# A hand-made order for the first projection of a hybrid encoder layer, its norm row spread by TensorE, and table powers moved from GpSimd to VectorE

## The chip, the cores and the metric

The kernel runs on one core of a Trainium2 chip. The metric is the device time of one execution in microseconds (us); the median of three runs is compared.

## The reference

One encoder layer is applied to a prompt of 256 and a sample of 1024 tokens, with a model width of 1024. Each row is normalized and projected by `w_in` into eight parts. `xs` goes through a bidirectional state-space mixer, q, k and v through differential attention; the rest are gates. Cut to what the change touches:

```python
h = x * rsqrt(mean(x * x) + eps) * norm_g            # (1280 tokens, 1024)
proj = h @ w_in                                      # xs, zs, q, k, v, za, gs, ga
A_bar = exp(A * dt)                                  # 2 directions, 32 groups, 64 states, complex
B_bar = (A_bar - 1) / A * B
h_f, h_b = scans with A_bar over (B_bar @ xs)        # forward and backward
y = real(C[0] @ h_f + C[1] @ h_b) + d_skip * xs
```

The kernel works in blocks of eight tokens. So it needs the powers of A_bar up to the eighth, and tables of the phase of A_bar to the eighth at each of 160 block positions. These tables are built as products of a low table (16 entries, `Tlr`, `Tli`) and a high one (10 entries, `Thr`, `Thi`).

## The kernel before

All matrix products are made of three fp32r products: each operand is split into a high part (a cast on ScalarE) and a low part (the rest, by a subtraction on VectorE or GpSimd).

The program goes through these phases. First the value projection: ten tiles of 128 tokens are loaded (`load_x`), normalized (`norm_x`), transposed on TensorE into `hTh` and `hTl` (`trans_x`), and multiplied by the value weights `Wvh` and `Wvl`, which come in four blocks of 128 columns (`load_wv`). The result goes through `vh` and `vl` to DRAM. The norm takes the sum of squares on ScalarE, some steps of one column on VectorE with a power on GpSimd between them (`rstd_newton`, L189 to L194), and one wide product with the row `gB`, which holds `norm_g` in all 128 partitions, loaded by a broadcast DMA. Second comes the xs projection (L572 to L586), third q and k with the rotary products (L605 to L630). Then follow the scans, attention, and the output stage.

Beside the first three phases a generator, `prep_gen`, makes the tables and the small matrices of the state-space part, one stretch of it at each `step_prep`. Its first part holds exponentials, sine and cosine, powers, and the tables; here `cmul(G, ...)` is six operations on GpSimd. Its loop of 16 rounds (from L390) begins behind the value projection, since its pool `prepl` stands on memory that this phase gives back. Each round makes `Bb` (GpSimd, L395 to L397), from it `Bm` (ScalarE, L401), `wbp` and `wc` (VectorE), four transposes of `wbp` (L413), small products with `Bb` and `Bm` (L435, L438), `kt`, and the wide table `tt` (GpSimd, L470).

A planner puts the instructions of every engine in order at build time, by priorities in program order and its own estimate of durations; on the chip each engine then works in that order and waits where an operand is late. `tc.issue_after(ins)` puts what is traced in it behind `ins` on the same engine. `tc.manual_schedule()` keeps the program's own order, on all engines or on those that are named; the scan phase already uses it for TensorE and SyncE. SyncE issues nearly all DMAs.

The pools that matter: `x` has three buffers, `vh` and `vl` one each, `wst` (raw weights) two, and `wh` and `wl` two each. PSUM has two banks for matmuls and two for transposes.

Of the kernel before, what the change touches and what calls it, by code (L numbers as in the profile page):

```python
# [11 lines left out]
F32 = mybir.dt.float32  # L12
F32R = mybir.dt.float32r
I32 = mybir.dt.int32
AF = mybir.ActivationFunctionType
ALU = mybir.AluOpType
AX = mybir.AxisListType
PSUM = bass.MemoryType.PSUM

D = 1024  # L20
KD = 8
DH = 512
# [21 lines left out]
PREPN = 2  # L44
PREP1 = 2
TTV = 0
GP = 1
O_XS, O_ZS, O_Q, O_K, O_V, O_ZA, O_GS, O_GA = 0, 512, 1024, 1536, 2048, 2560, 3072, 4096

# [60 lines left out]
def cmul(eng, o_re, o_im, a_re, a_im, b_re, b_im, t, u):  # L110
    eng.tensor_tensor(t, a_im, b_im, op=ALU.mult)
    eng.tensor_tensor(u, a_im, b_re, op=ALU.mult)
    eng.tensor_tensor(o_im, a_re, b_im, op=ALU.mult)
    eng.tensor_tensor(o_im, o_im, u, op=ALU.add)
    eng.tensor_tensor(u, a_re, b_re, op=ALU.mult)
    eng.tensor_tensor(o_re, u, t, op=ALU.subtract)
# [9 lines left out]
def kernel(  # L126
# [85 lines left out]

    wdma = [None]

    def w_stage(col, q=None):
        st = wp.tile([128, KD, 128], F32, tag="wst", name="wst")
        wdma[0] = (q or SP).dma_start(st, w_in_v[:, :, col:col + 128])
        return st

# [33 lines left out]
    def prep_gen():  # L253
# [79 lines left out]
        G.tensor_tensor(Gi, Gi, rc, op=ALU.mult)  # L333
        yield
        ua, ub = (cs, sn), (sc("ubr"), sc("ubi"))
        for _ in range(3):
            cmul(G, ub[0], ub[1], ua[0], ua[1], ua[0], ua[1], t1, t2)
            ua, ub = ub, ua
        ur, ui = ua
        uni = sc("uni")  # L340
        G.tensor_scalar(uni, ui, -1.0, None, op0=ALU.mult)
        Hr, Hi = sc("Hr"), sc("Hi")
        cmul(G, Hr, Hi, Gr, Gi, ur, uni, t1, t2)
        G.tensor_copy(ui[64:128], uni[64:128])
        yield
        Br = pp.tile([128, NG, GC], F32, name="Br")
        Bi = pp.tile([128, NG, GC], F32, name="Bi")
# [10 lines left out]
        for tr_, ti_, cnt in ((Tlr, Tli, 16), (Thr, Thi, 10)):  # L358
            G.memset(tr_[:, :, 0:1], 1.0)
            G.memset(ti_[:, :, 0:1], 0.0)  # L360
            n = 1
            while n < cnt:
                m = min(n, cnt - n)
                cmul(G, tr_[:, :, n:n + m], ti_[:, :, n:n + m], tr_[:, :, 0:m], ti_[:, :, 0:m],
                     bc(ur, 2, m), bc(ui, 2, m), bt[:, :, :m], bu[:, :, :m])
                cmul(G, wr, wi, ur, ui, ur, ui, t1, t2)
                ur, wr = wr, ur
                ui, wi = wi, ui
                n *= 2
                yield  # L370
# [108 lines left out]
    def step_prep(n=1, loop=True):  # L479
        for _ in range(n):  # L480
            if in_loop[0] and not loop:
                return
            if next(prep, None) == "loop":
                in_loop[0] = True

    with ExitStack() as p0:
        xp = p0.enter_context(tc.tile_pool(name="xp", bufs=2, reuse_waits="tile"))
        vp = p0.enter_context(tc.tile_pool(name="vp", bufs=1, reuse_waits="tile"))
        Wvh = vp.tile([128, KD, DH], F32R, name="Wvh")
        Wvl = vp.tile([128, KD, DH], F32R, name="Wvl")  # L490
        gB = vp.tile([128, D], F32, name="gB")
        xt = {}

        def load_x(i):
            t = xp.tile([128, D], F32, tag="x", name="x", bufs=3)
            for rs, src in x_rows(i):
                wdma[0] = SP.dma_start(t[rs], src)
            xt[i] = t

        xns = {}  # L500

        def norm_x(i):
            t = xt.pop(i)
            xn = xp.tile([128, D], F32, tag="xn", name="xn", bufs=2)
            ss = xp.tile([128, 1], F32, tag="ss", name="ss")
            r = xp.tile([128, 1], F32, tag="r", name="r")
            A.activation(xn, t, AF.Square, accum_out=ss)
            rstd_newton(xp, r, ss, D, EPS, "n")
            V.scalar_tensor_tensor(xn, t, r[:, 0:1], gB, op0=ALU.mult, op1=ALU.mult)
            xns[i] = xn  # L510

        def trans_x(i):
            xn = xns.pop(i)
            for hf in range(2):
                ps = tr_bank()
                for s in range(4):
                    k = hf * 4 + s
                    PE.transpose(ps[:, s * 128:(s + 1) * 128], xn[:, k * 128:(k + 1) * 128], ident)
                pv = ps.rearrange("p (k n) -> p k n", n=128)
                hs = (slice(None), slice(hf * 4, hf * 4 + 4), slice(i * 128, i * 128 + 128))  # L520
                A.copy(hTh[hs], pv)
                V.tensor_tensor(hTl[hs], pv, hTh[hs], op=ALU.subtract)

        def load_wv(b):
            st = w_stage(O_V + b * 128)
            A.copy(Wvh[:, :, b * 128:(b + 1) * 128], st)
            V.tensor_tensor(Wvl[:, :, b * 128:(b + 1) * 128], st, Wvh[:, :, b * 128:(b + 1) * 128], op=ALU.subtract)

        load_x(0)
        SP.dma_start(gB, norm_g[0:1].broadcast_to([128, D]))  # L530
        load_wv(0)
        load_wv(1)
        norm_x(0)
        trans_x(0)
        load_x(1)
        load_wv(2)
        load_wv(3)
        first = wdma[0]
        norm_x(1)
        for i in range(10):  # L540
            if i + 2 < 10:
                with tc.issue_after(first.ins):
                    load_x(i + 2)
                norm_x(i + 2)
            if i + 1 < 10:
                trans_x(i + 1)
            ps = mm_bank()
            tk = slice(i * 128, i * 128 + 128)
            hw = 256 if i < 2 else DH
            for c in range(0, DH, hw):  # L550
                cc = slice(c, c + hw)
                for k in range(KD):
                    PE.matmul(ps[:, cc], hTh[:, k, tk], Wvh[:, k, cc], start=(k == 0), stop=False)
                    PE.matmul(ps[:, cc], hTh[:, k, tk], Wvl[:, k, cc], start=False, stop=False)
                    PE.matmul(ps[:, cc], hTl[:, k, tk], Wvh[:, k, cc], start=False, stop=(k == KD - 1))
            vh = xp.tile([128, DH], F32R, tag="vh", name="vh", bufs=1)
            vl = xp.tile([128, DH], F32R, tag="vl", name="vl", bufs=1)
            A.copy(vh, ps)
            V.tensor_tensor(vl, ps, vh, op=ALU.subtract)
            for d_, s_ in ((vh_d, vh), (vl_d, vl)):  # L560
                SP.dma_start(d_[:, :, i, :].rearrange("h p e -> p h e"), s_.bitcast(F32).rearrange("p (h e) -> p h e", h=NH))
            with tc.issue_after(wdma[0].ins):
                step_prep(PREPN, False)

    with ExitStack() as p1:
        rp = p1.enter_context(tc.tile_pool(name="rp", bufs=1, reuse_waits="tile"))
# [620 lines left out]
```

## Time and profile before

| | us |
|---|---|
| median of 3 runs | 1134.97 |
| lowest and highest | 1134.88, 1136.84 |
| profiled execution | 1136.67 |
| its span, first to last instruction | 1134.9 |
| TensorE matmuls busy in it | 1069.3 |
| VectorE busy | 787.2 |
| ScalarE busy | 463.0 |
| GpSimd busy | 385.3 |

The rows below come from the profiled execution. PE is TensorE, PEld its weight loads, DVE VectorE, ACT ScalarE, POOL GpSimd, SPq the DMA issues of SyncE. An instruction row gives its start, its duration, the engine, the line, the operation with the tile it writes and the tiles it reads, partitions x elements, and a count; in brackets stands the idle time of the engine before it and what ended it. Consecutive matmuls overlap, so their pace is read from start to start.

### The profile page before, as it was taken

To read this page: it belongs to the slowest core of one execution; us is meant where nothing else is said; L and a number is where in the kernel's file an instruction comes from. 1 tells how busy PE (TensorE), PEld (TensorE's weight loads), DVE (VectorE), ACT (ScalarE), POOL (GpSimd) and SP (SyncE) were. 2 spreads that over 40 slices of the span, in tenths; PEclk is the share of its full clock that TensorE was granted. 3 is DMA by queue.
4 is the path that set the end of the run, shared out by engine and by line. 5 is a ranking of instruction groups with operands and counts; after the bars stand their busy time and mean duration, and the time that the engine had idled before them with its cause. 6 is when DMAs were issued, how large, how long until landed. Compare 5 with 4: busy or idle time off the path is not lost.

```text
span 1134.9 us, 18049 instructions
## 1 busy us (share of the span) xinstructions
PE 1069.3 (94%) x6475; PEld 989.2 (87%) x6475; DVE 787.2 (69%) x1458; ACT 463.0 (41%) x927; POOL 385.3 (34%) x551
## 2 busy tenths in 40 slices
PE   5998899999989999899999999999999999998997
PEld 4886677788889898799999998999999999998997
DVE  5856986997859999577678677766342676666524
ACT  4542332233212221355555555645453444544332
POOL 1499899922023323222122122222141003520032
PEclk8999899999998999999999999999999999999998
DMA  7934454555486765814525516311635974569212
GB/s 221 232 109 143 119 157 150 167 181 165 146 267 201 212 183 153 236 48 118 154 67 136 157 47 176 112 47 52 216 120 175 291 228 123 161 192 267 57 57 93
DMA packets 186297, 174.11 MB, mean 153 GB/s; under 512 B 32736, under 2 KB 161760, under 8 KB 186208
## 3 DMA queue, kind: packets, MB, share of 16 engines
q1 hardware_dynamic: 150880, 144.65, 43.2%
q10 hardware_dynamic: 35328, 28.32, 7.8%
q8 instruction: 51, 0.84, 0.3%
q14 instruction: 38, 0.31, 0.1%
HBM read 114.23 MB, written 58.69 MB: 152 GB/s over the span
## 4 chain that ended last, share of the span: by engine, by line
PE 45%; DVE 19%; DMA 7%; issue 4%; ACT 3%; POOL 3%; SPq 0%; POOLq 0%; ACTq 0%; DVEq 0%
PE mm L647 5%; PE mm L646 5%; PE mm L648 5%; DVE z L738 3%; DVE z L737 3%; PE xb L994 2%; PE xb L995 2%; PE xb L996 2%; PE tr L1127 2%; PE tr L1128 2%; PE tr L1129 2%; PE mm L245 2%; PE mm L247 2%; PE mm L246 2%; PE S L860 2%
## 5 line engine op out<-in xcount | busy, mean ns | idle before, releaser
L646 PE MATMUL mm<-hTh,wh 128*128 128x424 f32 (+1 forms) x576 | 213.0, 370 | 10.8 <-ACT zo L652 10.8
L648 PE MATMUL mm<-hTh,wl 128*128 128x424 f32 (+1 forms) x576 | 206.7, 359 | 0.0
L647 PE MATMUL mm<-hTl,wh 128*128 128x424 f32 (+1 forms) x576 | 206.6, 359 | 0.0
L646 PEld LDWEIGHTS mm<-hTh,wh 128*128 128x128 f32 x576 | 109.5, 190 | 17.4 <-ACT zo L652 13.0
L245 PE MATMUL mm<-hTh,wh 128*128 128x512 f32 (+1 forms) x288 | 107.5, 373 | 7.8 <-ACT xo L580 5.5
L647 PEld LDWEIGHTS mm<-hTl,wh 128*128 128x128 f32 x576 | 109.8, 191 | 4.6
L648 PEld LDWEIGHTS mm<-hTh,wl 128*128 128x128 f32 x576 | 109.5, 190 | 3.3
L864 DVE TENSOR_REDUCE mx<-S 128x1 f32<-128x1024 f32 (+1 forms) x80 | 84.3, 1058 | 38.8 <-PE S L862 38.5
L875 POOL TENSOR_SCALAR p<-p,rs 128x1024 f32<-128x1024 f32 (+1 forms) x40 | 41.5, 1037 | 202.2 <-DVE rs L873 196.3
L239 POOL TENSOR_TENSOR wl<-wst,wh 128x1024 fp32r<-128x1024 f32 x24 | 64.1, 2672 | 126.9 <-ACT wh L238 55.5
L246 PE MATMUL mm<-hTl,wh 128*128 128x512 f32 (+1 forms) x288 | 106.1, 368 | 0.0
L247 PE MATMUL mm<-hTh,wl 128*128 128x512 f32 (+1 forms) x288 | 104.2, 362 | 0.0
L868 ACT ACTIVATE p<-S,mx 128x1024 f32<-128x1024 f32 (+1 forms) x80 | 79.2, 993 | 59.9 <-DVE mx L865 47.1
L1127 PE MATMUL tr<-wqh,mh 128*128 128x256 f32 x320 | 89.7, 281 | 2.3 <-DVE o L1131 2.3
L1128 PE MATMUL tr<-wql,mh 128*128 128x256 f32 x320 | 89.2, 279 | 0.0
L1129 PE MATMUL tr<-wqh,ml 128*128 128x256 f32 x320 | 89.0, 279 | 0.0
L245 PEld LDWEIGHTS mm<-hTh,wh 128*128 128x128 f32 x288 | 55.3, 192 | 18.0 <-ACT xo L580 6.5
L1134 POOL TENSOR_TENSOR o<-o,finB 128x256 f32<-128x256 f32 x30 | 28.1, 938 | 104.9 <-ACT jk L1133 104.9
L1127 PEld LDWEIGHTS tr<-wqh,mh 128*128 128x128 f32 x320 | 60.1, 188 | 3.3 <-DVE o L1131 3.3
L246 PEld LDWEIGHTS mm<-hTl,wh 128*128 128x128 f32 x288 | 55.5, 193 | 8.6
L247 PEld LDWEIGHTS mm<-hTh,wl 128*128 128x128 f32 x288 | 55.2, 192 | 8.8
L1128 PEld LDWEIGHTS tr<-wql,mh 128*128 128x128 f32 x320 | 60.1, 188 | 0.0
(392 smaller groups left out, 2809.5 us busy)
## 6 DMA issues: line engine op xcount, KB each, us to landing
wst<-in_w_in_dram ACTq DMA_DIRECT2D x24, 512.0 KB, 3.9
wst<-in_w_in_dram SPq DMA_DIRECT2D x16, 512.0 KB, 5.5
wst<-in_w_branch_dram SPq DMA_DIRECT2D x32, 256.0 KB, 4.8
wqs<-in_w_out_dram SPq DMA_DIRECT2D x16, 512.0 KB, 4.3
tt_d<-tt SPq DMA_DIRECT2D x16, 320.0 KB, 2.6
tb<-tt_d SPq DMA_DIRECT2D x8, 640.0 KB, 4.5
zt<-gs_d SPq DMA_DIRECT2D x16, 320.0 KB, 4.1
x<-in_x_sample_dram SPq DMA_DIRECT2D x8, 512.0 KB, 5.1
```

The lines of the kernel that those rows point to most:

```text
L239: e.tensor_tensor(lv, st, hv, op=ALU.subtract)
L245: PE.matmul(ps[:, :n], wh[:, k, :], hTh[:, k, c0:c0 + n], start=(k == 0), stop=False)
L246: PE.matmul(ps[:, :n], wh[:, k, :], hTl[:, k, c0:c0 + n], start=False, stop=False)
L247: PE.matmul(ps[:, :n], wl[:, k, :], hTh[:, k, c0:c0 + n], start=False, stop=(k == KD - 1))
L646: PE.matmul(ps[:, :n], wh[:, k, :], hTh[:, k, c0:c0 + n], start=(k == 0), stop=False)
L647: PE.matmul(ps[:, :n], wh[:, k, :], hTl[:, k, c0:c0 + n], start=False, stop=False)
L648: PE.matmul(ps[:, :n], wl[:, k, :], hTh[:, k, c0:c0 + n], start=False, stop=(k == KD - 1))
L864: V.tensor_reduce(mx, S[:, :nk], axis=AX.X, op=ALU.max)
L868: A.activation(p[:, :nk], S[:, :nk], AF.Exp, bias=mx, scale=1.0 / math.sqrt(HD), accum_out=sm[:, t:t + 1])
L1127: PE.matmul(ps[:, :256], mh[:, k, ts_], oh_[:, k], start=(k == 0), stop=False)
L1128: PE.matmul(ps[:, :256], mh[:, k, ts_], ol_[:, k], start=False, stop=False)
L1129: PE.matmul(ps[:, :256], ml[:, k, ts_], oh_[:, k], start=False, stop=(k == 7))
```

## The change

The value projection is written out in a fixed order. Up to the split of the last weight block, all engines keep program order; behind that TensorE and SyncE do, and the others are planned, behind that split. The four weight blocks are asked for at once (two of them in the buffers of `wh` and `wl`), as are four x tiles. Block 1's low part is made on GpSimd. The first two tiles are multiplied by halves of the columns, the low halves first. `norm_g` is loaded as one row and spread over the partitions by two matmuls with a row of ones. There are 24 matmuls of `ones_e` with itself ahead of these and 30 behind, whose results nobody reads. The store of a tile's values is issued one round later, and `vh` and `vl` get two buffers. In `prep_gen` the three squarings and all powers for the low and the high table run on VectorE with temporaries of their own.

```diff
+WARM = 30
@@ prep_gen
+        v1, v2 = sc("v1"), sc("v2")
         for _ in range(3):
-            cmul(G, ub[0], ub[1], ua[0], ua[1], ua[0], ua[1], t1, t2)
+            cmul(V, ub[0], ub[1], ua[0], ua[1], ua[0], ua[1], v1, v2)
...
-        G.tensor_scalar(uni, ui, -1.0, None, op0=ALU.mult)
+        V.tensor_scalar(uni, ui, -1.0, None, op0=ALU.mult)
         Hr, Hi = sc("Hr"), sc("Hi")
         cmul(G, Hr, Hi, Gr, Gi, ur, uni, t1, t2)
-        G.tensor_copy(ui[64:128], uni[64:128])
+        sgn = sc("sgn")
+        V.tensor_copy(sgn[0:64], ui[0:64])
+        V.tensor_copy(sgn[64:128], uni[64:128])
+        u1r, u1i = sc("u1r"), sc("u1i")
+        V.tensor_copy(u1r, ur)
+        ur, ui, ub = u1r, sgn, (ur, ui)
...
-                cmul(G, tr_[:, :, n:n + m], ti_[:, :, n:n + m], tr_[:, :, 0:m], ti_[:, :, 0:m],
+                cmul(V, tr_[:, :, n:n + m], ti_[:, :, n:n + m], tr_[:, :, 0:m], ti_[:, :, 0:m],
                      bc(ur, 2, m), bc(ui, 2, m), bt[:, :, :m], bu[:, :, :m])
-                cmul(G, wr, wi, ur, ui, ur, ui, t1, t2)
+                cmul(V, wr, wi, ur, ui, ur, ui, v1, v2)
@@ value projection
-            t = xp.tile([128, D], F32, tag="x", name="x", bufs=3)
+            t = xp.tile([128, D], F32, tag="x", name="x", bufs=4)
...
-            V.scalar_tensor_tensor(xn, t, r[:, 0:1], gB, op0=ALU.mult, op1=ALU.mult)
+            w = D // 2 if i == 0 else D
+            for c in range(0, D, w):
+                V.scalar_tensor_tensor(xn[:, c:c + w], t[:, c:c + w], r[:, 0:1], gB[:, c:c + w], op0=ALU.mult,
+                                       op1=ALU.mult)
...
+        def split_wv(b, e):
+            st = wvs.pop(b)
             A.copy(Wvh[:, :, b * 128:(b + 1) * 128], st)
+            return e.tensor_tensor(Wvl[:, :, b * 128:(b + 1) * 128], st, Wvh[:, :, b * 128:(b + 1) * 128],
+                                   op=ALU.subtract)
...
-        SP.dma_start(gB, norm_g[0:1].broadcast_to([128, D]))
...
+        with tc.manual_schedule(engines={EN.PE, EN.SP}):
+            with tc.manual_schedule():
+                load_x(0)
+                g1 = xp.tile([1, D], F32, name="g1", bufs=1)
+                SP.dma_start(g1, norm_g[0:1])
+                wvs[0] = w_stage(O_V)
+                wvs[1] = w_stage(O_V + 128)
+                load_x(1)
+                wvs[2] = w_stage(O_V + 256, tag="wh")
+                wvs[3] = w_stage(O_V + 384, tag="wl")
+                load_x(2)
+                load_x(3)
+                one1 = xp.tile([1, 128], F32, name="one1", bufs=1)
+                V.memset(one1, 1.0)
+                junk = ps_w.tile([128, 512], F32, tag="junk", name="junk")
+                for _ in range(24):
+                    PE.matmul(junk[:, :128], ones_e, ones_e, start=True, stop=True)
+                for c in range(0, D, 512):
+                    ps = tr_bank()
+                    PE.matmul(ps, one1, g1[:, c:c + 512], start=True, stop=True)
+                    V.tensor_copy(gB[:, c:c + 512], ps)
+                for _ in range(WARM):
+                    PE.matmul(junk[:, :128], ones_e, ones_e, start=True, stop=True)
+                norm_x(0)
+                split_wv(0, V)
+                trans_x(0)
+                split_wv(1, G)
+                norm_x(1)
+                pss = [mm_bank()]
+                v_half(pss[0], 0, lo)
+                trans_x(1)
+                pss.append(mm_bank())
+                v_half(pss[1], 1, lo)
+                split_wv(2, V)
+                first = split_wv(3, V)
+            after_v = lambda: tc.issue_after(first.ins)
+            pend = []
+            for i in range(10):
+                if i + 4 < 10:
+                    load_x(i + 4)
+                with after_v():
+                    if i + 2 < 10:
+                        norm_x(i + 2)
+                    if 2 <= i + 1 < 10:
+                        trans_x(i + 1)
+                    if i < 2:
+                        v_half(pss[i], i, hi)
+                        ps = pss[i]
+                    else:
+                        ps = mm_bank()
+                        v_half(ps, i, slice(0, 512))
+                    pend.append(v_evict(ps, i))
+                    step_prep(PREPN, False)
+                if i:
+                    v_store(*pend.pop(0))
+            v_store(*pend.pop(0))
```

`v_half` makes the 24 matmuls of a tile over the given columns, `v_evict` the cast to `vh` and the subtraction to `vl`, and `v_store` the two stores; their bodies are those of the loop before.

## Rows read from the trace of the kernel before

**Rows 1.** Stretches: length, PE, PEld, DVE, ACT, POOL busy; granted clock, DMA share, GB/s

```profile
49.30:87.40 38.10, 38.08 (x184) 31.01 (x185) 20.63 (x44) 17.10 (x33) 37.91 (x116) 1.00 0.41 120
...
97.50:131.00 33.50, 24.42 (x118) 19.22 (x115) 27.87 (x46) 11.85 (x29) 29.38 (x63) 0.85 0.39 119
```

**Rows 2.** TensorE's waits, 86 to 231 us, and its wait for wbp, 96 to 126

```profile
PE tr L413 <- DVE wbp L116: 7.8, 3, 4.6
PE mm L245 <- ACT xo L580: 5.5, 3, 2.7
PE mm L245 <- DVE m L613: 2.3, 2, 1.8
PE tr L438 <- ACT Bm L401: 1.1, 1, 1.1
...
PE tr L413 <- DVE wbp L116: 6.5, 2, 4.6
```

**Rows 3.** ScalarE's longest wait, 86 to 231 us (total, times, longest)

```profile
ACT Bm L401 <- POOL Bb L116: 61.9, 11, 8.2
```

**Rows 4.** Timeline of a handover between GpSimd, ScalarE and VectorE

```profile
96.10 0.25 POOL L116 TENSOR_TENSOR Bb<-s,s 128x32 f32<-128x32 f32 x1
...
96.38 0.59 ACT L401 ACTIVATE Bm<-Bb,hmask 128x64 f32<-128x64 f32 x2 [8.17 <-POOL Bb L116]
...
98.82 3.03 DVE L239 TENSOR_TENSOR wl<-wst,wh 128x1024 fp32r<-128x1024 f32 x1 [3.94 <-ACT wh L238]
```

**Rows 5.** Timeline of the start, all engines

```profile
1.46 0.23 DVE L165 TENSOR_SCALAR ones_e<-ident 128x128 fp32r<-128x128 f32 x1
...
6.30 0.15 DVE L189 TENSOR_SCALAR nm<-ss 128x1 f32<-128x1 f32 x1 [4.61 <-ACT xn L507]
...
7.97 1.29 DVE L509 SCALAR_TENSOR_TENSOR xn<-x,r,gB 128x1024 f32<-128x1024 f32 x1
...
8.37 1.04 ACT L526 CAST Wvh<-wst 128x1024 fp32r<-128x1024 f32 x1 [2.10 <-DMA wst<-in_w_in_dram]
...
9.40 1.94 PE L518 MATMUL tr<-ident,xn 128*128 128x128 f32 x8 [9.40 <-DVE xn L509]
...
23.29 0.56 PE L554 MATMUL mm<-Wvl,hTh 128*128 128x256 f32 x1
...
23.64 0.41 PE L555 MATMUL mm<-Wvh,hTl 128*128 128x256 f32 x1
...
23.86 0.41 PE L553 MATMUL mm<-Wvh,hTh 128*128 128x256 f32 x1
...
30.00 0.28 PE L554 MATMUL mm<-Wvl,hTh 128*128 128x256 f32 x1
30.12 0.28 PE L555 MATMUL mm<-Wvh,hTl 128*128 128x256 f32 x1
```

**Rows 6.** GpSimd's timeline, a small and a wide table product, and a split

```profile
77.35 0.24 POOL L112 TENSOR_TENSOR t<-wi,wr 128x32 f32<-128x32 f32 x1
...
83.42 0.64 POOL L113 TENSOR_TENSOR Tli<-Tlr,wi 128x256 f32<-128x256 f32 x1
...
281.05 2.38 POOL L239 TENSOR_TENSOR wl<-wst,wh 128x1024 fp32r<-128x1024 f32 x1 [4.87 <-ACT wh L238]
```

**Rows 7.** VectorE's timeline, small and wide products

```profile
45.47 0.18 DVE L63 SCALAR_TENSOR_TENSOR xep<-xep,xer 128x32 f32<-128x32 f32 x1
45.57 0.18 DVE L101 TENSOR_TENSOR scsq<-scsq,scm 128x32 f32<-128x32 f32 x1
...
91.98 0.46 DVE L428 TENSOR_TENSOR d<-PCi,Cr 128x256 f32<-128x256 f32 x1
...
126.44 0.42 DVE L115 TENSOR_TENSOR e<-Fr,Br 128x256 f32<-128x256 f32 x1
...
130.16 0.95 DVE L111 TENSOR_TENSOR e<-Fi,Bi 128x256 f32<-128x256 f32 x1
```

**Rows 8.** TensorE's timeline, two fp32 products of 256 columns

```profile
174.67 1.13 PE L438 MATMUL tr<-wc,Bm 128*128 128x256 f32 x4
```

More of the change, by code (lines that the diff above doesn't have):

```diff
@@ L213, with w_stage @@
     wdma = [None]
-    def w_stage(col, q=None):
-        st = wp.tile([128, KD, 128], F32, tag="wst", name="wst")
+    def w_stage(col, q=None, tag="wst"):
+        st = wp.tile([128, KD, 128], F32, tag=tag, name="wst")
         wdma[0] = (q or SP).dma_start(st, w_in_v[:, :, col:col + 128])
@@ L492 @@
         xt = {}
+        ps_w = p0.enter_context(tc.tile_pool(name="ps_w", bufs=1, space=PSUM, reuse_waits="tile"))
+        EN = mybir.EngineType
         def load_x(i):
-            t = xp.tile([128, D], F32, tag="x", name="x", bufs=3)
+            t = xp.tile([128, D], F32, tag="x", name="x", bufs=4)
             for rs, src in x_rows(i):
@@ L522, in trans_x @@
                 V.tensor_tensor(hTl[hs], pv, hTh[hs], op=ALU.subtract)
-        def load_wv(b):
-            st = w_stage(O_V + b * 128)
+        def split_wv(b, e):
+            st = wvs.pop(b)
             A.copy(Wvh[:, :, b * 128:(b + 1) * 128], st)
-            V.tensor_tensor(Wvl[:, :, b * 128:(b + 1) * 128], st, Wvh[:, :, b * 128:(b + 1) * 128], op=ALU.subtract)
-        load_x(0)
-        SP.dma_start(gB, norm_g[0:1].broadcast_to([128, D]))
-        load_wv(0)
-        load_wv(1)
-        norm_x(0)
@@ L534 @@
[L534 to L547, printed above, removed]
-            tk = slice(i * 128, i * 128 + 128)
[L549 to L557, printed above, removed]
+            return e.tensor_tensor(Wvl[:, :, b * 128:(b + 1) * 128], st, Wvh[:, :, b * 128:(b + 1) * 128],
+                                   op=ALU.subtract)
@@ new lines, in v_half, with v_evict @@
+        def v_half(ps, i, cc):
+            tk = slice(i * 128, i * 128 + 128)
+            for k in range(KD):
+                PE.matmul(ps[:, cc], hTh[:, k, tk], Wvh[:, k, cc], start=(k == 0), stop=False)
+                PE.matmul(ps[:, cc], hTh[:, k, tk], Wvl[:, k, cc], start=False, stop=False)
+                PE.matmul(ps[:, cc], hTl[:, k, tk], Wvh[:, k, cc], start=False, stop=(k == KD - 1))
+        def v_evict(ps, i):
+            vh = xp.tile([128, DH], F32R, tag="vh", name="vh", bufs=2)
+            vl = xp.tile([128, DH], F32R, tag="vl", name="vl", bufs=2)
@@ L558, with v_store @@
             A.copy(vh, ps)
             V.tensor_tensor(vl, ps, vh, op=ALU.subtract)
+            return i, vh, vl
+        def v_store(i, vh, vl):
             for d_, s_ in ((vh_d, vh), (vl_d, vl)):
                 SP.dma_start(d_[:, :, i, :].rearrange("h p e -> p h e"), s_.bitcast(F32).rearrange("p (h e) -> p h e", h=NH))
-            with tc.issue_after(wdma[0].ins):
-                step_prep(PREPN, False)
+        wvs = {}
+        lo, hi = slice(0, 256), slice(256, 512)
+        with tc.manual_schedule(engines={EN.PE, EN.SP}):
[54 more added lines that the diff above has]
+            v_store(*pend.pop(0))
```

## Prediction

> **What bounds the kernel now.** I read the busy time by stretches first, then TensorE's list of waits, then the waits of ScalarE, and last the timelines around the stops. The first 87 us belong to the value projection, 87 to 176 to the xs projection, 176 to 309 to q and k; everything behind that is untouched and only shifts. In the projections TensorE is nearly always at work; what can be won are its stops. Two places have them.
>
> The first is the start: the first transposes come at 9.40, and the run without stops begins only with the matmul at 23.29 [rows 5]. From there to 87.4 TensorE is busy in 38.08 of the last 38.1 us [rows 1], so this phase has no other gap to give back.
>
> The second is the xs projection. From 97.5 to 131 TensorE is busy 24.42 of 33.5 us [rows 1], and its waits from 86 to 231 add up to 16.7 us [rows 2]. The releasers named are VectorE (wbp, 7.8 us), ScalarE (xo, 5.5 us; Bm, 1.1 us) and VectorE again (m, 2.3 us). Behind them stands GpSimd. ScalarE runs in order and waits 61.9 us in 11 waits for GpSimd's Bb, to make Bm [rows 3]. The handover shows how this spreads: Bb ends at 96.35, Bm starts at 96.38, the cast of the next weights sits behind it on ScalarE, and VectorE has idled 3.94 us when it can begin its half of the split at 98.82, which takes 3.03 us [rows 4]; its wbp products come after that. GpSimd is late because it is full: 37.91 of 38.1 us busy from 49.3 to 87.4, and 29.38 of 33.5 from 97.5 on [rows 1], and the power tables lie in its queue ahead of and between the Bb.
>
> **The change, part by part.** *Powers on VectorE.* Removed from GpSimd: 18 products of three squarings, one negation, one half copy, and eight rounds of the tables, each with 6 small products and 6 table products. That is 68 operations of 128x32 at 0.24 us, 16.3 us, and table products of 32, 64, 128 and 256 columns (12, 18, 12 and 6 of them). With 0.24 us at 32 and 0.64 at 256 columns [rows 6], and straight lines between (0.30 and 0.41, estimates), they take 2.9 + 5.4 + 4.9 + 3.8 = 17.0 us. GpSimd's queue gets 33 us shorter, and Bb no longer waits behind it.
>
> On VectorE the 128x32 operations start 0.10 us apart, and 128x256 takes 0.42 [rows 7]. Its share is 70 small ones, 7.0 us, and 1.2 + 2.6 + 2.8 + 2.5 = 9.1 us of table products (0.144 and 0.24 for 64 and 128 columns, estimates between the same ends): 16.1 us. They land between 49.3 and 87.4, where VectorE is idle 38.1 - 20.63 = 17.5 us [rows 1]; this slack hides them. Without it they would cost TensorE up to 16 us. Beside GpSimd the price grows: a 128x256 product takes 0.46 us beside its small operations and 0.95 beside the wide ones [rows 7]. In this stretch GpSimd has mostly small ones, so I take 0.46 / 0.42, a factor 1.1: 17.7 us. That fills the slack to the brim, and since the tables are wanted only later, I charge 1 us (between 0 and the 19.5 us of the slower rival below).
>
> The Trainium skill, "GPSIMD Engine Reference", section "Key points", says that the engine shares its SBUF interfaces with VectorE and contends with VectorE instructions that read two SBUF inputs, which all the moved products do. The trace agrees for the wide operations: 0.95 against 0.42 us [rows 7]. If it held as fully for the narrow ones, the sum would be that of rival D.
>
> *What the xs phase gets back.* Of TensorE's 16.7 us, the waits for xo (5.5), for Bm (1.1) and the two of wbp that fall between 96 and 126 (6.5 of the 7.8) have a late Bb at their head: 13.1 us [rows 2]. If Bb is early, ScalarE's casts and evictions go out in time, and VectorE starts its splits without those idle spells. Not all of it comes back: VectorE is busy 27.87 of 33.5 us there [rows 1], and wide GpSimd work now runs beside it from the start of the phase. I take 10 of 13.1 (bounds 0 and 13.1), and 1 us (0 to 2) for the half clock after the longest stop: the granted clock of 97.5 to 131 is 0.85 [rows 1].
>
> *The start.* Removed is the 512 KB broadcast load of gB; added are a 4 KB load, two matmuls against a row of ones and two VectorE copies, which stand ahead of the norm of tile 0 in a fixed order, behind 24 warm-up matmuls. No row shows a 128-column fp32r matmul. From above, a cold transposition of 128 columns takes 1.94 / 8 = 0.24 us; from below, half of a cold 256-column matmul (0.22 apart) is 0.11 [rows 5]. I take 0.13, nearer to the like kind: 24 of them end 3.1 us after ones_e is ready at 1.69, at 4.8. Four passes of fp32 over 256 columns took 1.13 us at full clock [rows 8], which is two products, so 512 columns take about 1.0, and up to 2.0 cold; I take 1.6 each: 8.0. The copy of a half, priced as half of the 1.29 us product xn, adds 0.65: 8.7, where the first step of the norm stood at 6.30 [rows 5]. So the norm slips by 2.4 us to 10.4, its first half ends at 11.0, and 30 more warm-ups (3.9 us) end at 11.9. Transposes of tile 0 then start at 11.9 instead of 9.40.
>
> From there: transposes 1.5 (0.8 to 1.94), the casts of hTh behind them 0.6, the cast of block 1 on ScalarE 1.04 [rows 5], its low part on GpSimd 2.38 [rows 6], so 17.4; the half tile of 24 matmuls at 0.12 to 0.22 apart [rows 5], 4 us, so 21.4; transposes of tile 1 and its first casts 1.9: 23.3. What is left for TensorE then equals what was left at 23.29 before. Bounds: every price at its low end gives 18.8, every one at its high end 32.7. What is gained is the clock: 15 matmuls from 23.64 ran 0.22 apart instead of 0.12 [rows 5], 1.5 us, as TensorE will then have been at work since 17.4. Against it stands 0.4 us, since the splits of blocks 2 and 3 now follow on VectorE. Start: 1 us gained (6 gained to 9 lost).
>
> The Trainium skill, "TensorE: Matmul & The Clock Gate", Part 1, has the default state throttled and activity releasing it. By that alone the warm-ups let the half tile and the transposes of tile 1 take 2.9 and 0.8 us, and the start gains 2.2 us more. The rows show both paces [rows 5]; the 4 us nearly without a matmul in my sum, while block 1 is split, speak against it.
>
> *Fixed order on TensorE and SyncE; loads.* TensorE can no longer fill a gap of the value projection with other work, but it hardly did: it had none. Four blocks and four x tiles are asked for at once, so the later splits no longer wait for a load; VectorE's order decides there, so I add nothing. On SyncE a store moves behind the next x load, which is hidden by four x buffers. The small tables' loads keep their places between x loads, more than 10 us ahead of use.
>
> Sum: 1 (start) + 10 + 1 (xs) - 1 (VectorE) = 11 us. The profiled execution took 1136.67 us, of which 1134.9 are the span and 1.8 lie around it; 11 less is 1125.7. The median of the runs is 1134.97, 1.7 below the profiled one, so the forecast of the median is 1124.
>
> **Rivals.**
> A, everything works: the start comes in near its low bound (4 us more) and the xs phase gives back all 13.1 and 2. For it: all those waits have one head. Against it: VectorE's load. Time 1124 - 4 - 4 = 1116; chance 0.13.
> B, GpSimd's lateness hid a second bound: once Bb is early, VectorE, 27.87 / 33.5 = 83% busy there [rows 1], becomes the releaser of the same stops. Then only about 3 us come back: 1132. Chance 0.15.
> C, nothing: the new order of the start loses what the tables win, 1135. Chance 0.08.
> D, slower: VectorE becomes late within the value projection, 49 to 87. If the factor beside GpSimd is 0.95 / 0.42 = 2.3 there too, the tables take 37 us, 19.5 over the slack, and TensorE in its fixed order waits with it: 1135 - 12 + 19.5 = 1142.5. It decides from a factor of (17.5 + 12) / 16.1 = 1.8. For it: products with two inputs; against it: GpSimd has fewer wide operations there. Chance 0.14.
> The forecast, 1119 to 1130, has 0.50.
>
> **How the numbers follow.** Measurement tells 0.2% (2.3 us) from no change. Faster holds the forecast, A and B: 0.78; same C: 0.08; slower D: 0.14. The range from 1114 to 1137 leaves out D and the outer half of A: about 2 in 10.
>
> **What would show it.** Right: ScalarE's wait for Bb below 20 us, no stop of TensorE over 2 us between 97 and 131 (shifted), GpSimd idle before the value projection ends, TensorE's unbroken run beginning near 23. Wrong: stops of TensorE before 87 released by xn or hTl; the first half tile waiting past 20 for block 1; the same stops in the xs phase with VectorE always busy.

## The result, and the profile of the changed kernel

The changed kernel took 1146.3 us (median of 4 runs, 1144.32 to 1148.77) against 1134.93 for the kernel before (4 runs): a ratio of 1.0089, with a 95% interval of 1.0072 to 1.0106. It is slower by about 10 us; forecast were 1124 us and a range up to 1137. The profiled execution took 1144.32 us, its span is 1142.4.

**The start.** The timeline of the changed kernel, TensorE and VectorE and the waits that matter (start, duration, engine, operation, and in brackets the idle time ahead and what ended it). It answers to [rows 5].

```profile
1.74 5.38 PE L579 MATMUL junk<-ones_e 128*128 128x128 f32 x24 [1.74 <-DVE ones_e L166]
...
7.05 3.78 PE L582 MATMUL tr<-g,one 1*128 1x512 f32 x4
...
10.76 6.66 PE L585 MATMUL junk<-ones_e 128*128 128x128 f32 x30
10.86 0.69 DVE L583 COPY gB<-tr 128x512 f32<-128x512 f32 x1 [1.02 <-PE tr L582]
...
11.47 0.14 DVE L190 TENSOR_SCALAR nm<-ss 128x1 f32<-128x1 f32 x1
...
13.13 1.42 DVE L521 SCALAR_TENSOR_TENSOR xn<-x,r,gB 128x512 f32<-128x512 f32 x2
...
17.22 1.93 PE L531 MATMUL tr<-ident,xn 128*128 128x128 f32 x8
...
23.20 0.58 PE L547 MATMUL mm<-Wvl,hTh 128*128 128x256 f32 x1 [1.85 <-POOL Wvl L540]
...
23.58 0.41 PE L548 MATMUL mm<-Wvh,hTl 128*128 128x256 f32 x1
23.79 0.41 PE L546 MATMUL mm<-Wvh,hTh 128*128 128x256 f32 x1
...
30.29 0.39 PE L546 MATMUL mm<-Wvh,hTh 128*128 128x256 f32 x1 [0.24 <-ACT hTh L534]
...
31.36 0.28 PE L547 MATMUL mm<-Wvl,hTh 128*128 128x256 f32 x1
31.48 0.28 PE L548 MATMUL mm<-Wvh,hTl 128*128 128x256 f32 x1
```

The warm-ups take 0.22 us each, 12.0 us in all. The norm row's two products (1.9 us each) stand behind the first 24, the norm of tile 0 behind the copies of the row, and its transposes behind the last 30: the tile was ready at about 14.6, the transposes come at 17.22. They still run at 1.93 us for eight, the pace of before, and the first half tile, which waits until 23.20 for the low part of block 1, at 0.21 us a matmul. The first half of tile 1 begins at 30.29; its matmuls start 0.12 us apart from 31.24 on, but further stops follow (below). The kernel before began its unbroken run at 23.29 [rows 5].

**The value projection.** Busy time by stretches, first of the changed kernel, then of the kernel before (length, then PE, PEld, DVE, ACT, POOL busy; granted clock, DMA share, GB/s):

```profile
50.00:75.00 25.00, 24.71 (x128) 20.39 (x127) 24.37 (x109) 15.38 (x31) 18.50 (x49) 1.00 0.61 137
75.00:100.00 25.00, 22.44 (x100) 18.35 (x99) 20.15 (x96) 3.91 (x7) 0.65 (x2) 0.93 0.24 74
```

```profile
50.00:75.00 25.00, 25.00 (x125) 20.68 (x126) 16.30 (x37) 14.75 (x29) 24.81 (x76) 1.00 0.45 130
75.00:100.00 25.00, 23.85 (x116) 19.04 (x115) 12.22 (x24) 6.30 (x11) 25.00 (x78) 1.00 0.41 127
```

VectorE is now full between 50 and 75, where it had 8.7 us to spare, and GpSimd does nearly nothing between 75 and 100. TensorE's list of waits from 20 to 100 us in the changed kernel (total, times, longest):

```profile
PE tr L531 <- DVE are L277: 2.6, 1, 2.6
PE tr L531 <- DVE nm L190: 2.6, 1, 2.6
PE mm L547 <- POOL Wvl L540: 1.9, 1, 1.9
```

The second of these ends at 80.22. VectorE's timeline of the changed kernel shows what stood there, table products between the steps of a norm:

```profile
74.98 0.14 DVE L192 TENSOR_TENSOR nm<-nm,nl 128x1 f32<-128x1 f32 x1
...
75.36 0.28 DVE L112 TENSOR_TENSOR bt<-Tli,sgn 128x128 f32<-128x128 f32 x1
...
77.23 0.14 DVE L195 TENSOR_TENSOR r<-nm,nl 128x1 f32<-128x1 f32 x1
77.30 1.27 DVE L535 TENSOR_TENSOR hTl<-tr,hTh 128x512 fp32r<-128x512 f32 x2
...
78.80 1.27 DVE L521 SCALAR_TENSOR_TENSOR xn<-x,r,gB 128x1024 f32<-128x1024 f32 x1
```

The last value matmul starts at 99.8, against 87.2 before: 12.6 us later.

**The xs phase.** TensorE's waits from 99 to 239 us, ScalarE's longest wait there, and GpSimd's timeline where the loop begins; these answer to [rows 2 to 4].

```profile
PE tr L420 <- DVE wbp L117: 3.1, 1, 3.1
PE mm L246 <- ACT xo L635: 2.9, 2, 1.5
PE tr L442 <- DVE kt L452: 2.5, 1, 2.5
PE mm L246 <- DVE m L668: 1.9, 2, 1.3
```

```profile
ACT Bm L408 <- POOL Bb L117: 61.9, 12, 8.7
```

```profile
100.31 0.25 POOL L112 TENSOR_TENSOR s<-Bi,Gi 128x32 f32<-128x32 f32 x1 [19.46 <-PE mm L548]
```

TensorE's stops fall from 16.7 to 12.7 us, and ScalarE still waits 61.9 us for Bb. GpSimd, with its tables gone, stood idle 19.46 us and began the loop only when the last value matmul had ended. From there the gap to the kernel before closes from 12.6 us to 8.5 at the first product of q with the cosine table (191.5 against 183.0), and the span ends 7.5 later.

### The profile page after: what moved, and what is told of

The parts are those of the page before. It is cut to its first block, busy times and chain, and to the rows that moved or that the text cites. A ratio compares the mean times of both kernels' runs of the same rounds, so it can differ in the third digit from the quotient of the medians.

```text
span 1142.4 us, 18163 instructions
## 1 busy us (share of the span) xinstructions
PE 1084.5 (95%) x6533; PEld 1002.8 (88%) x6533; DVE 804.7 (70%) x1579; ACT 463.0 (41%) x927; POOL 354.3 (31%) x436
## 4 chain that ended last, share of the span: by engine, by line
PE 43%; DVE 17%; DMA 10%; ACT 4%; issue 3%; POOL 3%; SPq 1%; POOLq 0%; ACTq 0%; DVEq 0%
PE mm L701 5%; PE mm L702 5%; PE mm L703 5%; PE mm L246 3%; PE mm L248 2%; PE mm L247 2%; DVE z L793 2%; DVE z L792 2%; DMA wqs<-in_w_out_dram 2%; PE S L915 2%; PE tr L940 2%; PE S L917 2%; PE xb L1049 2%; PE xb L1050 2%; PE xb L1051 2%
## 5 line engine op out<-in xcount | busy, mean ns | idle before, releaser
L930 POOL TENSOR_SCALAR p<-p,rs 128x1024 f32<-128x1024 f32 (+1 forms) x40 | 41.5, 1038 | 204.1 <-DVE rs L928 193.2
L1183 PE MATMUL tr<-wql,mh 128*128 128x256 f32 x320 | 89.2, 279 | 0.0
```

The lines of the kernel that those rows point to most:

```text
L1183: PE.matmul(ps[:, :256], mh[:, k, ts_], ol_[:, k], start=False, stop=False)
```

## The experiments

Each kernel was timed beside the kernel before on the same chip; its ratio is to those runs. "Value" is the start of the last value matmul, "q" the first product with the cosine table, "xs" what lies between, and "scan" the start of the first matmul of the scans, behind which nothing was edited; all are us from the trace.

| kernel | median us | ratio, 95% interval | value | q | xs | scan |
|---|---|---|---|---|---|---|
| before | 1134.93 to 1137.73 | 1 | 87.2 | 183.0 | 95.8 | 322.4 |
| changed | 1146.3 | 1.0089, 1.0072 to 1.0106 | 99.8 | 191.5 | 91.7 | 329.0 |
| e1 powers only | 1141.08 | 1.0022, 1.0008 to 1.0036 | 100.1 | 193.2 | 93.1 | 328.8 |
| e2 powers back | 1147.31 | 1.0077, 1.0049 to 1.0104 | 97.7 | 190.8 | 93.1 | 331.0 |
| e3 no warm-ups | 1138.45 | 1.0007, 0.9987 to 1.0028 | 97.1 | 190.4 | 93.3 | 325.8 |
| e4 row by DMA | 1139.57 | 1.0012, 0.9995 to 1.0029 | 97.8 | 191.2 | 93.4 | 326.3 |
| e5 order alone | 1138.61 | 1.0017, 1.0002 to 1.0032 | 93.6 | 188.5 | 94.9 | 324.3 |
| e6 copies off ScalarE | 1139.60 | 1.0027, 1.0010 to 1.0043 | 97.6 | 188.8 | 91.2 | 324.9 |
| e7 few products | 1123.37 | 0.9886, 0.9861 to 0.9911 | 89.8 | 177.5 | 87.7 | 311.1 |
| e8 powers left out | 1130.41 | 0.9937, 0.9917 to 0.9956 | 88.0 | 179.5 | 91.5 | 315.7 |
| e9 half on VectorE | 1131.48 | 0.9957, 0.9938 to 0.9975 | 92.3 | 180.5 | 88.2 | 319.4 |
| e10 warm-ups only | 1139.72 | 1.0029, 1.0011 to 1.0046 | 93.8 | 187.6 | 93.8 | 328.1 |
| e11 order, TensorE planned | 1136.57 | 1.0009, 0.9992 to 1.0026 | 89.6 | 182.3 | 92.7 | 321.6 |
| e12 one round a tile | 1143.68 | 1.0077, 1.0052 to 1.0102 | 98.8 | 187.9 | 89.1 | 329.9 |
| e13 other half | 1141.12 | 1.0029, 1.0014 to 1.0045 | 97.2 | 190.6 | 93.4 | 325.8 |
| e14 order and half | 1135.68 | 0.9982, 0.9966 to 0.9998 | 92.9 | 185.8 | 92.9 | 322.0 |
| e15 order planned, half | 1132.33 | 0.9946, 0.9922 to 0.9970 | 90.3 | 179.5 | 89.2 | 317.7 |

Each edit also gives the planner another order on the engines that it plans, so 2 or 3 us in one column need no cause in the edit; I build on larger ones and on stops that the trace names. Of the columns it is "scan" that the times follow: by it and by the ratio, a kernel's distance from the kernel before differs by 4 us at most. A lateness at "value" or "q" is in part made up again (e1 is 12.9 us late at the first, 10.2 at the second, 6.4 at the scans, and 2.5 by the ratio).

### The change taken apart: e1 to e4

**e1**, the kernel before with the powers on VectorE, and nothing else:

```diff
-            cmul(G, ub[0], ub[1], ua[0], ua[1], ua[0], ua[1], t1, t2)
+            cmul(V, ub[0], ub[1], ua[0], ua[1], ua[0], ua[1], v1, v2)
...
-                cmul(G, tr_[:, :, n:n + m], ti_[:, :, n:n + m], tr_[:, :, 0:m], ti_[:, :, 0:m],
+                cmul(V, tr_[:, :, n:n + m], ti_[:, :, n:n + m], tr_[:, :, 0:m], ti_[:, :, 0:m],
...
-                cmul(G, wr, wi, ur, ui, ur, ui, t1, t2)
+                cmul(V, wr, wi, ur, ui, ur, ui, v1, v2)
```

> The kernel before, with the powers on VectorE and nothing else of the change. Theory 1 (the powers help by themselves, all of the loss comes from the new order of the value projection): value projection ends near 87.4 us as before, the xs phase gives back about 4 us and q and k about 3, as the changed kernel showed; 1128 to 1131 us. Rival (the powers make VectorE late inside the value projection, and this is where the change loses): the value projection ends 4 or more us later, 1136 to 1142 us.

Slower by 0.2%, the rival's side. Its busy time by stretches, and TensorE's waits from 50 to 98 us:

```profile
50.00:75.00 25.00, 17.49 (x76) 13.74 (x76) 23.09 (x87) 11.35 (x23) 17.57 (x45) 0.83 0.38 111
75.00:100.00 25.00, 23.70 (x108) 18.89 (x107) 15.86 (x76) 5.55 (x10) 0.55 (x1) 0.96 0.21 64
```

```profile
PE tr L524 <- DVE hTl L528: 4.6, 2, 3.5
PE mm L559 <- ACT hTh L527: 4.3, 2, 4.0
```

VectorE is full between 50 and 75 again, and TensorE stops for the casts of the transposed tile. Between 75 and 100 VectorE has 9 us left over, and GpSimd is idle.

**e2**, the changed kernel with the powers on GpSimd again (the lines of e1's diff reversed):

> The changed kernel, with the powers back on GpSimd. Theory 1: the start stays as late (first half tile of tile 1 near 30 us), the stop of 2.6 us at 77 us goes, but the xs phase loses its 4 us and q and k their 3; 1148 to 1153 us. Rival: without the powers VectorE is in time in the value projection, which ends 5 us earlier than 100 us; 1138 to 1143 us.

1.0077: nearly all of the loss stays, and the xs phase loses 1.4 us of the 4 that theory 1 expected. In the presence of the rest of the change the powers' place is worth 0.1%, within the intervals.

**e3**, the changed kernel without the 54 warm-ups:

```diff
-WARM = 30
+WARM = 0
...
-                for _ in range(24):
+                for _ in range(0):
```

> The changed kernel without its 24 and 30 warm-up matmuls; the norm row is still spread by TensorE. Theory 1 (the warm-ups, 0.22 us each, only hold up the spreading of the row, the norm and the first transposes, and do not raise the clock): transposes of tile 0 start near 11.3 us instead of 17.2, the half tile of tile 1 near 24.4 instead of 30.3, 1139 to 1141 us. Rival (what the start gains is lost again behind it, as VectorE sets the pace of the first tiles): less than 2 us, 1144.5 us or more.

**e4**, the same, with the norm row by the broadcast load of the kernel before:

```diff
-                g1 = xp.tile([1, D], F32, name="g1", bufs=1)
-                SP.dma_start(g1, norm_g[0:1])
+                SP.dma_start(gB, norm_g[0:1].broadcast_to([128, D]))
...
-                for c in range(0, D, 512):
-                    ps = tr_bank()
-                    PE.matmul(ps, one1, g1[:, c:c + 512], start=True, stop=True)
-                    V.tensor_copy(gB[:, c:c + 512], ps)
```

> The changed kernel without the warm-ups and with the norm row loaded by the broadcast DMA of before. Theory 1: the norm of tile 0 starts near 5.7 us instead of 11.5, its transposes near 9 us, the half tile of tile 1 near 22 us, 1136 to 1139 us. Rival: as for the run without warm-ups, 1144.5 us or more.

Without warm-ups the ratio falls from 1.0089 to 1.0007: they are the larger part of the loss, some 9 us of 10 by the two ratios (6 to 12 with their intervals). The transposes of tile 0 then start at 11.4 instead of 17.2, and the first half of tile 1 at 26.2 instead of 30.3, later than the 24.4 expected. The trace places only a part of the 9 us: 2.7 at the end of the value projection, 3.2 at the scans, 5.4 over the span. With the powers on GpSimd (e2 against e5, where the way of the norm row differs too) it is 6.7 at the scans, and 0.6% in the ratios. The way of the norm row makes no difference that shows (1.0007 and 1.0012), though tile 0 comes at 8.6 in e4.

### Warm-ups and order by themselves: e10, e5, e11

**e10**, the kernel before with 30 warm-ups where TensorE is idle anyway:

```diff
+        for _ in range(30):
+            PE.matmul(junk[:, :128], ones_e, ones_e, start=True, stop=True)
         load_x(0)
```

> The kernel before with 30 of the warm-up matmuls and nothing else of the change; at 0.22 us each they run from 1.7 to 8.3, ahead of the first transposes at 9.4, so that nothing waits for them. Theory 1 (they don't change TensorE's pace): the first eight transposes take 1.94 us again, the first half tile runs at 0.21 us a matmul, and the time is that of the kernel before within 1.5 us. Rival (they raise the pace, and the loss in the changed kernel came only from their standing in front of the norm row): the transposes take 1.0 us, the half tile runs at 0.12, and the time is 2 to 4 us less.

TensorE's timeline of e10:

```profile
1.74 6.66 PE L532 MATMUL junk<-ones_e 128*128 128x128 f32 x30 [1.74 <-DVE ones_e L165]
9.17 1.94 PE L518 MATMUL tr<-ident,xn 128*128 128x128 f32 x8 [0.76 <-DVE xn L509]
...
20.65 0.37 PE L557 MATMUL mm<-Wvh,hTh 128*128 128x256 f32 x1
20.86 0.28 PE L558 MATMUL mm<-Wvl,hTh 128*128 128x256 f32 x1
20.98 0.28 PE L559 MATMUL mm<-Wvh,hTl 128*128 128x256 f32 x1
```

The pace is as theory 1 has it: the transposes behind the warm-ups take 1.94 us, and matmuls start 0.21 us apart until 20.86, then 0.12, the two levels of 1.2 and 2.4 GHz. In the kernel before, without any warm-ups, a first run of matmuls 0.12 us apart comes sooner, behind 17.48:

```profile
17.59 0.28 PE L554 MATMUL mm<-Wvl,hTh 128*128 128x256 f32 x1
17.70 0.29 PE L555 MATMUL mm<-Wvh,hTl 128*128 128x256 f32 x1
```

The time of e10 was missed: 0.3% slower. Its new plan has stops of 5.2 us on hTh and 3.7 on hTl. So the warm-ups bought no earlier pace here; that they cost by themselves, out of the way, this run doesn't settle.

The Trainium skill, "TensorE: Matmul & The Clock Gate", Part 1, has sustained activity of TensorE release its throttle. Neither 6.7 us of warm-ups here nor the 12 us of the changed kernel did that for the transposes that followed.

**e5**, the new order alone: e4 with the powers on GpSimd.

> The new order and the loads of four blocks and four x tiles, without warm-up matmuls, with the norm row by the broadcast load, and with the power tables on GpSimd as before. Theory 1 (the power tables on VectorE are what stops the value projection, the order itself costs nothing): the value projection ends at 87 to 91, as in the kernel before, the xs phase keeps its stops, and the time is 1133 to 1139. Rival (the fixed order itself costs, since TensorE stands at the head of its list whenever a norm or a cast comes late): the value projection ends at 95 or later even so, and the time is 1139 to 1143.

**e11**, e5 with TensorE's order left to the planner:

```diff
-        with tc.manual_schedule(engines={EN.PE, EN.SP}):
+        with tc.manual_schedule(engines={EN.SP}):
```

> The run with the order alone, with TensorE left to the planner (SyncE keeps the written order). Theory 1 (the 6.4 us by which the value projection ended later there come from what VectorE holds ahead of the norms and casts, the exponential above all): TensorE's stops between 20 and 40 stay at 5 us or more, the projection ends at 92 to 95, and the time is 1136 to 1140. Rival (the written order of TensorE makes them, since other ready matmuls may not fill in): the stops fall under 3 us, the projection ends at 86 to 90, and the time is 1130 to 1134.

e5 is 0.2% slower; its 1138.6 us lie at the upper end of theory 1's range, and the value projection ends at 93.6, between the two. TensorE's waits of e5 from 15 to 100 us:

```profile
PE tr L525 <- DVE xep L64: 3.9, 1, 3.9
PE mm L542 <- DVE hTl L529: 2.4, 1, 2.4
PE mm L541 <- POOL Wvl L534: 1.8, 1, 1.8
```

All three lie ahead of 36 us; the first is an exponential for the tables on VectorE, ahead of a norm. From 50 to 93 TensorE never stops. With TensorE planned, 4 of the 6.4 us come back (89.6), and the time is that of the kernel before within its interval. e11 met neither theory cleanly: 25 us of 30 are busy between 20 and 50, so the stops stay at 5.3 us, as theory 1 said, but the phase ends as the rival said.

### Where the powers' gain went: e6, e8, e7

**e6**, e1 with the copies PB and PC on GpSimd, followed a guess from e1's trace, that ScalarE's copies, which wait for GpSimd's Pi, hold up the casts of hTh:

```diff
-            A.copy(pb_[0:64], p_[0:64, 7::-1, :])
+            G.tensor_copy(pb_[0:64], p_[0:64, 7::-1, :])
```

and the other three lines alike.

> The kernel before with the powers on VectorE, and the eight copies PB and PC on GpSimd instead of ScalarE. Theory 1 (in the run with the powers alone the value projection ended 12.9 us later because ScalarE stood 5.3 us in front of the powers of Pi, with the casts of hTh behind the copies): the stops of 4.0 and 3.5 us before 72 go, the value projection ends at 89 to 94, and the time is 1131 to 1136, below the kernel before. Rival (VectorE itself is late beside GpSimd, and the transposes wait for hTl whatever ScalarE does): the value projection still ends at 97 or later, and the time stays 1138 to 1142.

The guess fell. The value projection ends at 97.6, and TensorE now waits 5.3 us for VectorE's hTl at once (until 69.47). VectorE's timeline of e6 ahead of that, with powers from 64.00 to 68.74:

```profile
65.59 0.72 DVE L114 TENSOR_TENSOR sgn<-sgn,v 128x32 f32<-128x32 f32 x1
...
68.74 0.68 DVE L528 TENSOR_TENSOR hTl<-tr,hTh 128x512 fp32r<-128x512 f32 x1
```

**e8**, the kernel before without the eight rounds of powers (nobody computes them):

```diff
-                cmul(G, tr_[:, :, n:n + m], ti_[:, :, n:n + m], tr_[:, :, 0:m], ti_[:, :, 0:m],
-                     bc(ur, 2, m), bc(ui, 2, m), bt[:, :, :m], bu[:, :, :m])
-                cmul(G, wr, wi, ur, ui, ur, ui, t1, t2)
```

> The kernel before with the eight rounds of powers left out (the tables are filled with constants, so the output lacks them): nothing takes their 33 us of GpSimd over. It gives the upper bound of what moving them can bring. Theory 1 (the xs phase gives back 4 us or so, since GpSimd is full there anyway): 1128 to 1133. Rival (the prediction's step, 11 us given back once the tables are out of GpSimd's queue): 1121 to 1127.

Even for nothing the powers are worth 0.6% (0.4 to 0.8), 7 us by the ratio, 4.3 of them in the xs phase: less than the 11 forecast for it. GpSimd's timeline of e8 shows one reason:

```profile
88.23 0.48 POOL L111 TENSOR_TENSOR s<-Bi,Gi 128x32 f32<-128x32 f32 x1 [14.06 <-PE mm L548]
```

As in the changed kernel, GpSimd stood idle, here 14.06 us, until the last value matmul (88.0) and only then began the loop. In the code the loop's buffers are opened behind the value projection; the trace names that matmul as what ended the wait. The first product of Bb came at 89.05 in e8, 1.1 us behind the last value matmul, and at 91.74 in the kernel before, 4.5 us behind it (87.2): the tables had delayed the start of the loop by some 3.5 us. The other reason stands in ScalarE's timeline, here the second and third round of Bm, first of the kernel before, then of e8:

```profile
103.20 0.59 ACT L401 ACTIVATE Bm<-Bb,hmask 128x64 f32<-128x64 f32 x2 [3.45 <-POOL Bb L116]
...
111.60 0.59 ACT L401 ACTIVATE Bm<-Bb,hmask 128x64 f32<-128x64 f32 x2 [5.46 <-POOL Bb L116]
```

```profile
104.92 0.59 ACT L395 ACTIVATE Bm<-Bb,hmask 128x64 f32<-128x64 f32 x2 [5.89 <-POOL Bb L116]
...
116.04 0.59 ACT L395 ACTIVATE Bm<-Bb,hmask 128x64 f32<-128x64 f32 x2 [4.37 <-POOL Bb L116]
```

In the kernel before, GpSimd works on the tables until 114.4, between the products of Bb. In e8 the planner puts the loop's wide products (h and tt, 0.9 to 1.1 us each) in their place: GpSimd is busy 41.77 of the 42 us from 88 to 130, and the first Bb come no earlier. Of TensorE's waits from 86 to 231 us, those for xo (5.5 us before) and wbp (7.8) shrink, but stay:

```profile
PE mm L245 <- ACT xo L574: 4.2, 2, 2.5
PE tr L407 <- DVE wbp L116: 3.2, 1, 3.2
```

**e7**, the kernel before with two of the six wide products of each tt:

```diff
-            cmul(V if pb % 8 < TTV else G, sp(tt[:, 0]), sp(tt[:, 1]), bc(Thr[:, gs], 3, 16), bc(Thi[:, gs], 3, 16),
-                 bc(Tlr[:, gs], 2, 10), bc(Tli[:, gs], 2, 10), sp(h1), sp(h2))
+            G.tensor_tensor(sp(tt[:, 0]), bc(Thr[:, gs], 3, 16), bc(Tlr[:, gs], 2, 10), op=ALU.mult)
+            G.tensor_tensor(sp(tt[:, 1]), bc(Thi[:, gs], 3, 16), bc(Tlr[:, gs], 2, 10), op=ALU.mult)
```

> The kernel before with 4 of the 6 wide products of each tt left out (the output then lacks them); the power tables stay on GpSimd. Theory 1 (GpSimd's own work in each turn of the loop, tt above all, sets when the next Bb comes, so that the tables ahead of it are not the cause of the stops in the xs phase): TensorE's waits for wbp, xo and Bm fall from 13 to under 6 us, and the time is 1122 to 1129. Rival (the prediction's step: the late start of the loop, behind the tables, makes the stops): the stops stay at 10 us or more, and the time is 1132 to 1136.

1.1% faster, and of the stops in the xs phase two kinds are left. TensorE's waits of e7 from 86 to 231 us:

```profile
PE mm L245 <- ACT xo L580: 3.5, 2, 2.0
PE tr L413 <- DVE wbp L116: 2.8, 2, 1.7
```

6.3 us instead of 16.7 [rows 2], a little over the expected 6. So the loop's own wide products on GpSimd keep Bb late too. But e7 and e8 don't set one task of GpSimd against the other: over the execution GpSimd is busy 327.5 us in e7 and 358.1 in e8, against 385.3 before, and by the ratios e7 gains 12.9 us for 57.8 and e8 7.2 for 27.2, about 0.2 to 0.3 us for each us taken off GpSimd in both.

### By place or by number: e9, e13, e12

**e9**, the kernel before with only the last four rounds on VectorE:

```diff
-                cmul(G, tr_[:, :, n:n + m], ti_[:, :, n:n + m], tr_[:, :, 0:m], ti_[:, :, 0:m],
+                E = V if tr_ is Thr else G
+                cmul(E, tr_[:, :, n:n + m], ti_[:, :, n:n + m], tr_[:, :, 0:m], ti_[:, :, 0:m],
...
```

The rounds on VectorE have temporaries of their own.

> The kernel before with only the last four rounds of powers (those of Thr and Thi, 48 operations) on VectorE. Theory 1 (the moved operations cost by the place where they stand in VectorE's queue: those that fall behind 75, where VectorE was busy 12.2 of 25 us, are hidden, those between 50 and 75 are not): the value projection ends at 87 to 90, the xs phase gives back 2 to 3 us, and the time is 1132 to 1136, 0.1 to 0.4% below the kernel before. Rival (whatever runs on VectorE beside a busy GpSimd makes the casts of hTl late, wherever it stands): the value projection ends at 92 or later, and the time is 1137 to 1140.

**e13**, its complement: the squarings and the first four rounds on VectorE, the last four on GpSimd.

> The complement of the run with half of the powers: the three squarings and the first four rounds (Tlr, Tli) on VectorE, the last four rounds (Thr, Thi) on GpSimd. Theory 1 (place: these operations fall between 50 and 75, where VectorE is already busy 16.3 of 25 us, and stand ahead of the casts of hTl): TensorE has stops of 4 us or more on hTl between 55 and 75, the value projection ends at 95 or later, and the time is 1137 to 1142. Rival (number: half as many operations on VectorE do half the harm, wherever they stand, so this run is like the other half): the value projection ends at 91 to 94 and the time is 1131 to 1135.

Busy time by stretches, first e9, then e13:

```profile
50.00:75.00 25.00, 24.27 (x121) 19.79 (x122) 16.16 (x36) 14.76 (x29) 23.86 (x76) 1.00 0.46 136
75.00:100.00 25.00, 23.14 (x98) 18.44 (x97) 18.07 (x57) 6.32 (x14) 20.13 (x57) 0.93 0.36 111
```

```profile
50.00:75.00 25.00, 18.01 (x73) 14.09 (x72) 23.74 (x89) 10.57 (x22) 17.15 (x42) 0.80 0.34 98
75.00:100.00 25.00, 24.61 (x115) 19.68 (x114) 11.73 (x23) 7.88 (x12) 16.53 (x51) 1.00 0.24 73
```

The signs are those of theory 1. The last rounds fall behind 75, where VectorE rises from 12.2 to 18.1 of 25 us and stays below full; the kernel is 0.4% faster. The first ones fall between 50 and 75, fill VectorE to 23.7 of 25, and TensorE stops 3.7 us for hTl (4 or more were expected) and 3.3 for hTh; the kernel is 0.3% slower. So the place of the operations counts. The two parts are not of one size, though: 48 operations in e9, 70 in e13. How much of the difference is the place alone isn't shown. One part of e9's expectation was missed: its value projection ends at 92.3, not by 90, and the xs phase gives back 7.6 us, not 2 or 3; I can't say why it gives back more than in e8.

**e12** was to spread the powers of e1:

```diff
-                step_prep(PREPN, False)
+                step_prep(PREPN if i < 3 else 1, False)
```

> The run with the powers alone on VectorE, with one step of the tables for each token tile from tile 3 on instead of two, so that the powers are spread over more tiles and the last rounds reach into the xs phase. Theory 1 (the powers hurt because they stand bunched ahead of the casts, 23 of 25 us between 50 and 75): the stops of 4.0 and 3.5 us shrink to under 2 each, the value projection ends at 88 to 93; the loop starts later, so the xs phase gives back less, and the time is 1133 to 1139. Rival (contention with GpSimd makes each operation dear, spread or not): the value projection ends at 97 or later, and the time is 1140 or more.

It met the rival's numbers, but does not speak for the rival: VectorE was busy 24.06 of 25 us between 50 and 75, so the planner had put the powers in the same place as in e1, and nothing was spread.

### Together: e14 and e15

e5 and e11, each with the last four rounds on VectorE as in e9:

> The run with the order alone, and the last four rounds of powers on VectorE. Theory 1 (the two add up: the order costs 0.2%, the half saves 0.4%): 1132 to 1136. Rival (in the written order VectorE's later norms make TensorE stand, so that the half costs as the whole did): 1138 to 1143.

> The same with TensorE left to the planner. Theory 1 (they add up: 0.1% and less 0.4%): 1130 to 1135, and the value projection ends at 88 to 93. Rival (the half gains only in the plan of the kernel before): 1136 to 1140.

Both add up as theory 1 said. e14, with the written order, is 0.2% faster than the kernel before, and e15, which leaves TensorE to the planner, 0.5%. e15 and e9 beat both kernels; their intervals overlap, so which is better stays open.

## Why the prediction was wrong

It was on the wrong side: two steps failed, that VectorE's slack hides the powers and that a late Bb goes with them, and two terms of the start were mis-sized.

**The start** was to gain 1 us, with bounds from 6 gained to 9 lost. Its anchors came late: transposes at 17.22 instead of 11.9, the run of full pace at 30.29 instead of 23.3, near the high bound of 32.7. Mis-sized were the warm-up (0.22 us for 0.13; I took half of a cold 256-column matmul as the nearer row, and the cold transposition at 0.24 was the right one) and the row's product (1.9 for 1.6). The clock gain of 1.5 us came, as the matmuls from 31.24 on start 0.12 us apart, but it stands against 7 us by which the anchor at 23.3 was missed. e3 shows the price by the time: without the warm-ups the loss is gone to within the interval, though its trace is still 3.4 us late at the scans.

**Powers on VectorE.** The failed step is "this slack hides them". The price was nearly right: 17.7 us were put down; in e1 VectorE is busy 10.8 us more between 20 and 100 (66.95 against 56.19), and 7.8 us of wbp and wc products that the kernel before did there have moved behind it, so the powers took about 19, 1.2 times the 16.1 without GpSimd beside them. But 17.5 us of slack between 49 and 87 were counted as one sum, where 8.7 of 25 us were free up to 75 and the rest later. The chain of powers is ready early, stands in VectorE's queue ahead of norms and casts, and fills the first part; e9 and e13 show both parts of that. I charged 1 us; the value projection ended 12.9 later in e1, and 2.1 and 4.3 later beside the new order (the changed kernel against e2, e4 against e5). Rival D named the place and the sign, but its cause, a price of 2.3 times, is not what the runs show: single operations of 32 columns do take up to 0.76 us, yet their sum stays near the price. That its 1142.5 us lie near the 1146.3 measured is luck, as most of that loss comes from the warm-ups.

**What the xs phase gets back.** The step that failed is that "Bb no longer waits behind" the tables, at 10 + 1 us. With the eight rounds left out and nothing in their place, the xs phase gives back 4.3 us and the whole kernel 7 (e8); in the changed kernel it is 4.1. The start of the loop was held by the end of the value projection and only some 3.5 us by the tables, and behind that the loop's own wide products fill the time that the tables leave, so Bb stays late. Of the three kinds of wait that I put under a late Bb, which total 14.4 us in the kernel before with all of wbp, 8.9 remain in e8 (xo 4.2, wbp 3.2, Bm 1.5), and waits for kt and wbt (3.6) come up instead. The marks that I had set say so: ScalarE's wait is 61.9 us, not under 20. That GpSimd would be idle ahead of the end of the projection was right, and worth nothing.

**Fixed order at nothing** was too low by little: 0.2% with TensorE written by hand (e5), nothing that shows with TensorE planned (e11).

The sum from the runs: the order alone 0.2%, all the powers on top of it nothing that shows (e4 against e5, where the value projection ends 4.3 us later and the xs phase gives back 1.5), the warm-ups 0.6 to 0.8% (e2 less e5, the changed kernel less e3).

## What to carry to other kernels

Idle time of an in-order engine is no single sum: before work is moved into it, see in which 10 or 20 us the free time lies, when the moved work becomes ready, and what stands behind it in the queue; the last 48 operations of this work, which fell where there was room, gained 0.4%, the first 70, which fell where there was little, lost 0.3%. Ask when the engine that is relieved can use its time: here its next work was held until the last value matmul. Two cheap kernels, one with the work left out and one with its neighbour thinned, would have told what a microsecond off GpSimd is worth, here 0.2 to 0.3 us, before 11 us were put down for 33.

## What the runs showed of the hardware

- 54 matmuls of 128 columns from 1.74 to 17.42 us, 0.22 us each, were followed by eight transposes in 1.93 us, as without any; the pace of 256-column matmuls went from 0.21 to 0.12 us only later (at 20.86 in e10; in the kernel before, without any, at 17.48).
- The granted clock reads 1.00 for the stretch from 0 to 20 us in e10 while its matmuls run at the lower pace, so ahead of the first change the pace has to be read from the matmuls.
- In the changed kernel, between 71.7 and 75.0, beside GpSimd's 256-column products of F, every second VectorE product of 32 or 64 columns takes 0.73 to 0.89 us, and those between them 0.18 to 0.22. The Trainium skill, "GPSIMD Engine Reference", section "Key points", has the two engines contend over their SBUF interfaces for instructions with two SBUF inputs; the trace agrees for single operations, with this size.
